# Three written-out engine orders replaced by others in a one-core attention kernel

## The chip, the cores and the metric

The kernel runs on one core of one Trainium2 chip. The metric is the device time of one execution in microseconds (us). Three timed runs of the kernel before gave 189.55, 189.56 and 189.82 us, with a median of 189.56 us.

## The reference

Cosine attention over 8 batches and 12 heads, 512 positions, head dimension 64, all in float32 in HBM:

```
Q_norm = Q / (norm(Q) + 1e-10);  K_norm = K / (norm(K) + 1e-10)
scores = Q_norm @ K_norm.T / tau            # tau = 0.1
weights = softmax(scores)                   # over the keys
out = weights @ V
```

## The kernel before

**Tiles.** Two neighbouring heads of one batch make a *pair*; there are 48 pairs, numbered 0 to 47. Each pair has four *chunks* of 128 keys, numbered 0 to 3. I write (42,2) for chunk 2 of pair 42. Each pair goes through these operations; the name in capitals is the key that the code gives it, and the line is where its instruction is issued.

- LD and LV (L311, L314): loads of Q, K and V, issued by SyncE.
- SQ (L337): GpSimd squares Q and K of a pair, one instruction of 128x1024.
- SSQ (L354) and RED (L361, L365): the sums of squares. For most pairs K's are first folded by eight matmuls with the identity (SSQ, written beside the outputs in one of the two `ops` banks of PSUM) and then reduced by a short VectorE instruction (L361). Q's are reduced by a long VectorE instruction alone (L365).
- NEW (L389 to L403): eight or nine small VectorE instructions that make 1/norm by Newton steps for a whole group of pairs at once. From pair 20 on a group has four pairs; group 18 is pairs 44 to 47. NEW18.7 is step 7 of group 18.
- SCL (L420): Q and K times 1/norm, to bf16. Q's (SCL s.0) on VectorE, K's (SCL s.1) mostly on GpSimd.
- TR (L426): four TensorE transposes each for Q (TR s.0) and K (TR s.1) into the one PSUM tile `tps`. EVA (L434): VectorE copies the tile to SBUF as `qt`. The next pair's TR can only start when EVA has emptied the tile.
- SCO (L508): two matmuls of 64x512 give the scores of one chunk for both heads, into one of two halves of `scps`. The halves alternate, so the scores of a chunk wait for the exponential of the chunk two before.
- EXP (L531): ScalarE's exponential of one chunk, 128x1024, from `scps` to `et`. For the last chunk of pair 47 there are three pieces (L522).
- VC (L536): GpSimd converts V to bf16 in `vb`, with a column of ones beside it.
- PV (L548; L576 for pair 47): the outputs. PV s.h.i is the group of four matmuls that sums head h and query tile i over the four chunks. It needs all four exponentials of its pair, VC, and an emptied `ops` bank.
- RCP and NRM (L559, L561): VectorE divides by the sums of weights and empties the bank. ST (L565): the store, issued by SyncE.

Two chunks, (37,3) and (45,3), get their exponential from a polynomial and not from ScalarE (function `poly`). Their scores (SCX, L468) go to `tps`; X (L473, L475) runs on VectorE; four steps Y s.0 to Y s.3 (L479, L480) on GpSimd; the last two, Y s.4 (L486) and Y s.5 (L480), on VectorE. Both of these last two read two tiles in SBUF.

**Order of the work.** Nothing in the program decides at run time. `P.add` collects 1831 operations in a list, and `ORDER` gives for each engine a string of indices into that list. `schedule` (L33) turns the strings into queues, and `run` (L43) writes each queue with a semaphore wait ahead of every operation whose inputs come from another engine. Each engine is strictly in order: an operation that waits holds up all behind it on its engine. How far operations may run ahead is set by the rings of buffers (L622): 15 pairs of Q, K and `vb`, 10 of V, 6 of squares, 4 of `qn`, `qt` and `et`, 8 of outputs.

A *slot* in what follows is TensorE's stretch between two neighbouring SCO in its queue; slot (42,2) is the one that ends with SCO of (42,2). The other TensorE work, PV, TR and SSQ, stands in slots.

Of the kernel before, what the change touches and what calls it, by code (L numbers as in the profile page):

```python
# [639 lines left out]
def slack(s, most):  # L640
# [14 lines left out]
    ),  # L655
    "pool": (
# [7 lines left out]
    ),  # L664
    "dve": (
# [24 lines left out]
    ),  # L690
# [33 lines left out]
    ),  # L724
    "act": (
# [44 lines left out]
```

## Time and profile before

| | |
|---|---|
| median of 3 runs | 189.56 us |
| the profiled execution's own time | 189.84 us |
| its span | 187.9 us |
| granted TensorE clock | 1.00 |
| ScalarE, TensorE, VectorE, GpSimd busy | 180.8, 173.7, 172.3, 166.8 us |
| HBM traffic | 50.3 MB, 268 GB/s over the span |

The page of the profile gives busy time by engine, the chain of work that ended last and the costliest groups. The timeline view lists single instructions or runs of equal ones as start, length, engine, line, operation, tiles and count; a bracket at the end tells idle time of the engine just before the row and who ended it. The records of one engine overlap: an instruction of ScalarE or VectorE is shown as started while the one before it still drains. So what an instruction occupies is read from start to start or from end to end, not from its length.

### The profile page before, as it was taken

The numbers are of one execution on the slowest core, as the hardware profiler recorded it, in microseconds if no ns is written. First come the engines' busy times: TensorE is split into PE (matmuls) and PEld (weight loads), VectorE is DVE, ScalarE is ACT, GpSimd is POOL, SyncE is SP. The second block draws the span as 40 slices with busy tenths as digits, with TensorE's granted clock in tenths as the row PEclk, the third lists the DMA queues.
The fourth block names the chain that finished last, engine by engine and source line by source line (L and its number), as shares of the span: only waits on it lengthen the run. The fifth ranks groups of instructions, "written<-read, shape, count | busy, mean of one in ns | idle before, by whom it ended". The sixth has DMA issues, their size and how long they took to land.

```text
span 187.9 us, 6635 instructions
## 1 busy us (share of the span) xinstructions
PE 173.7 (92%) x2694; PEld 108.7 (58%) x2694; DVE 172.3 (92%) x546; ACT 180.8 (96%) x212; POOL 166.8 (89%) x152
## 2 busy tenths in 40 slices
PE   6999999999998999999999999899999989999983
PEld 2655666566665666666666556556645446655552
DVE  2789999999999999999999999999999999988864
ACT  4799999999999999999999999999999999999992
POOL 4797999999999999999999999999999999696600
PEclk9999999999999999999999999999999999999999
DMA  4999999899999988999999999976996551312215
GB/s 148 356 350 349 348 354 331 233 328 370 379 385 375 326 243 264 333 304 297 361 379 381 380 380 301 306 244 198 302 336 194 173 167 59 112 59 76 95 59 169
DMA packets 52446, 50.76 MB, mean 270 GB/s; under 512 B 3136, under 2 KB 52416, under 8 KB 52416
## 3 DMA queue, kind: packets, MB, share of 16 engines
q1 hardware_dynamic: 51984, 50.02, 81.1%
q8 instruction: 21, 0.34, 0.8%
q10 hardware_dynamic: 432, 0.33, 0.5%
q14 instruction: 9, 0.07, 0.1%
HBM read 37.75 MB, written 12.58 MB: 268 GB/s over the span
## 4 chain that ended last, share of the span: by engine, by line
ACT 92%; PE 4%; DMA 1%; DVE 1%; issue 1%; POOL 0%
ACT et L531 90%; DMA qk<-in_Q_dram 1%; PE ops L548 1%; PE scps L508 1%; DVE xs L245 0%; PE ops L576 0%; ACT ys L379 0%; DVE ob L589 0%; PE scps L268 0%; POOL qn L258 0%; ACT nps L382 0%; PE tps L268 0%; ACT sq L239 0%; ACT et L522 0%; PE scps L194 0%
## 5 line engine op out<-in xcount | busy, mean ns | idle before, releaser
L531 ACT ACTIVATE et<-scps 128x1024 bf16<-128x1024 f32 (+1 forms) x191 | 174.3, 1151 | 0.5 <-PE scps L508 0.5
L337 POOL TENSOR_TENSOR sq<-qk 128x1024 bf16<-128x1024 f32 x44 | 82.7, 1893 | 1.4 <-DMA qk<-in_K_dram 1.2
L508 PE MATMUL scps<-qt 64*128 64x512 bf16 x380 | 75.2, 386 | 7.8 <-ACT et L531 4.4
L548 PE MATMUL ops<-vb,et 128*128 128x65 bf16 x1504 | 71.6, 194 | 1.1 <-DVE qn L420 0.5
L548 PEld LDWEIGHTS ops<-vb,et 128*128 128x128 bf16 x1504 | 55.1, 98 | 27.1 <-issue 17.4
L420 POOL TENSOR_TENSOR qn<-qk,rk 128x512 bf16<-128x512 f32 x36 | 37.2, 1042 | 2.8 <-DVE rk L394 2.5
L561 DVE TENSOR_TENSOR ob<-ops,rd 128x256 f32<-128x256 f32 x94 | 38.9, 417 | 0.4
L420 DVE TENSOR_TENSOR qn<-qk,nps 128x512 bf16<-128x512 f32 x58 | 38.5, 677 | 0.4 <-ACT nps L382 0.4
L434 DVE COPY qt<-tps 128x1024 bf16<-128x1024 bf16 x47 | 32.3, 687 | 2.6 <-PE tps L426 2.1
L426 PE MATMUL tps<-ident,qn 128*128 128x128 bf16 x376 | 33.9, 221 | 0.1
L508 PEld LDWEIGHTS scps<-qt 64*128 64x128 bf16 x380 | 18.9, 92 | 26.0 <-ACT et L531 11.8
L365 DVE TENSOR_REDUCE nps<-sq 128x8 f32<-128x512 bf16 x48 | 32.3, 683 | 0.0
L536 POOL TENSOR_SCALAR vb<-vf 128x512 bf16<-128x512 f32 x48 | 30.8, 655 | 0.2
L426 PEld LDWEIGHTS tps<-ident,qn 128*128 128x128 bf16 x376 | 21.4, 98 | 12.9 <-issue 6.6
L559 DVE RECIPROCAL rd<-ops 128x4 f32<-128x4 f32 x94 | 16.2, 176 | 3.3 <-PE ops L548 2.3
L354 PE MATMUL ops<-sq,ident 128*128 128x64 bf16 x368 | 18.5, 194 | 0.0
L354 PEld LDWEIGHTS ops<-sq,ident 128*128 128x128 bf16 x368 | 13.9, 98 | 4.1 <-issue 2.7
L361 DVE TENSOR_REDUCE nps<-ops 128x8 f32<-128x64 f32 x40 | 8.5, 213 | 0.6 <-PE ops L354 0.5
L389 DVE TENSOR_TENSOR nps<-nps,ys 128x32 f32<-128x32 f32 (+1 forms) x30 | 6.3, 209 | 0.1
L390 DVE SCALAR_TENSOR_TENSOR nps<-nps,ys 128x32 f32<-128x32 f32 (+1 forms) x30 | 6.2, 208 | 0.1
L480 POOL TENSOR_TENSOR xz<-xz 128x1024 f32<-128x1024 f32 x2 | 3.8, 1892 | 1.5 <-DVE xz L475 1.5
L191 PE MATMUL ops<-warm_in,ident 128*128 128x512 bf16 x8 | 3.6, 628 | 1.4 <-POOL ident L181 1.4
(61 smaller groups left out, 65.0 us busy)
## 6 DMA issues: line engine op xcount, KB each, us to landing
vf<-in_V_dram SPq DMA_DIRECT2D x48, 256.0 KB, 5.8
qk<-in_Q_dram SPq DMA_DIRECT2D x47, 256.0 KB, 5.0
qk<-in_K_dram SPq DMA_DIRECT2D x47, 256.0 KB, 5.7
out_dram<-ob SPq DMA_DIRECT2D x47, 256.0 KB, 3.9
qk<-in_Q_dram SPq DMA_DIRECT2D x2, 128.0 KB, 2.7
qk<-in_K_dram ACTq DMA_DIRECT2D x2, 128.0 KB, 2.9
out_dram<-ob SPq DMA_DIRECT2D x1, 128.0 KB, 1.7
out_dram<-ob ACTq DMA_DIRECT2D x1, 64.0 KB, 1.6
```

Source lines behind the costliest of these rows:

```text
L337: lambda e: e.tensor_tensor(out=sqf, in0=data, in1=data, op=ALU.mult))
L354: last = e.matmul(out=o_ps[bank][:, 320:384], lhsT=ident[:, :], rhs=sq[iqs][:, 8 * w : 8 * w + 8, 8 * k : 8 * k + 8], start=(k == 0), stop ...
L365: lambda e, w=w, dst=dst: e.tensor_reduce(out=dst, in_=sq[iqs][:, 8 * w : 8 * w + 8, :], axis=AX.X, op=ALU.add))
L420: lambda e, w=w, r=r: e.tensor_tensor(out=qn[iqn][:, w].rearrange("p t h d -> p h t d"), in0=qk[iq][:, w].rearrange("p h (t d) -> p h t d" ...
L426: last = e.transpose(t_ps[:, w, t, :], qn[iqn][:, w, t].rearrange("p h d -> p (h d)"), ident[:, :])
L434: lambda e: e.tensor_copy(out=qt[iqt][:, :, :, :].rearrange("p w t x -> p (w t x)"), in_=t_ps[:, :, :, :].rearrange("p w t x -> p (w t x)")))
L508: last = e.matmul(out=sc_ps[:, 2 * b + h, :], lhsT=qt[iqt][64 * h : 64 * h + 64, 1, c, :], rhs=qt[iqt][64 * h : 64 * h + 64, 0, :, :], sta ...
L531: lambda e, c=c, b=b, hs=hs: e.activation(out=et[iet][:, c, hs[0] : hs[-1] + 1, :], in_=sc_ps[:, 2 * b + hs[0] : 2 * b + hs[-1] + 1, :], f ...
L536: lambda e: e.tensor_scalar(out=vb[:, iq, :, :, 0:DIM].rearrange("p c h d -> p h c d"), in0=vf[iv][:, :, :].rearrange("p h (c d) -> p h c ...
L548: last = e.matmul(out=o_ps[h][:, 65 * t : 65 * t + 65], lhsT=et[iet][:, c, h, 128 * t : 128 * t + 128], rhs=vb[:, iq, c, h, :], start=(c = ...
L559: lambda e, h=h, grid=grid: e.reciprocal(out=rd[io][:, h, :], in_=grid[:, :, DIM]))
L561: lambda e, h=h, grid=grid: e.tensor_tensor(out=ob[io][:, h], in0=grid[:, :, 0:DIM], in1=rd[io][:, h, :].unsqueeze(2).to_broadcast([128, N ...
```

## The change

Three of the five strings in `ORDER` are replaced: those of GpSimd, VectorE and TensorE. SyncE's and ScalarE's strings, the operations themselves, their needs and all buffers stay as they are, and each new string has the same indices as the old one, in another order. In the queues the first difference is at SQ 21 on GpSimd, at NRM 12.0 on VectorE and at TR 15.0 on TensorE, some 58 to 62 us into the span; 79 of 148 places differ on GpSimd, 252 of 546 on VectorE and 419 of 735 on TensorE.

The change describes itself as orders of pairs 16 and later searched anew, with later scores and the lock of GpSimd and VectorE in the sum (that is, in the search's own cost), and with each query tile's values over all chunks in a row.

The diff, cut to parts that the prediction speaks of. GpSimd, around the polynomial of pair 37 (1436 to 1439 are Y37.0 to Y37.3; 1442, 1509, 1552 and 1476 are VC of pairs 37, 39, 40 and 38; 1684 is SCL 44.1):

```diff
-        "1176 1310 1459 1569 1210 1343 1603 1253 1526 1287 1386 1321 1397 1354 1421 1637 1670 1465 1712 1436 1437 "
-        "1438 1439 1476 1442 1509 1575 1552 1791 1586 1757 1609 1642 1740 1620 1684 1719 1653 1763 1774 1809 1695 "
-        "1796 1734 1735 1736 1737 "
+        "1493 1176 1242 1343 1310 1459 1569 1603 1397 1442 1526 1287 1386 1421 1637 1509 1321 1354 1465 1670 1712 "
+        "1436 1437 1438 1439 1552 1476 1575 1791 1609 1740 1757 1774 1642 1809 1695 1620 1586 1684 1719 1763 1796 "
+        "1653 1734 1735 1736 1737 "
```

TensorE, lines with pairs 40 to 42 (1612 is SCO (42,0), 1614 SCO (42,1), 1616 SCO (42,2); 1685 and 1683 are TR 44.1 and TR 44.0; 1553 to 1561 are PV of pair 40):

```diff
-        "1516 1517 1518 1519 1584 1641 1553 1643 1554 1612 1559 1560 1614 1555 1561 1562 1685 1683 1616 1556 1618 "
+        "1516 1517 1518 1519 1553 1584 1643 1641 1612 1554 1555 1559 1560 1561 1614 1685 1683 1616 1556 1562 1618 "
```

In the same way, slot by slot, with the operations named:

| slot | before | after |
|---|---|---|
| (26,1) | TR27.0, PV25.0.0, PV25.0.1 | PV24.1.2, PV24.1.3, TR27.0 |
| (28,2) | PV27.0.0 to 27.0.3, SSQ34.1 | PV27.1.0, PV27.0.0 |
| (30,1) | PV29.0.0, PV29.1.0 | TR31.1 |
| (40,2) | PV38.0.0 to 38.0.3, SSQ45.1 | PV38.0.0 to 38.0.3, SSQ45.1, PV38.1.0 |
| (40,3) | TR41.1, PV38.1.0 | nothing |
| (41,0) | five PV | six PV |
| (41,1) | PV39.0.3, PV38.1.3, SSQ46.1, TR42.1 | PV39.0.3, SSQ46.1 |
| (42,0) | TR43.0, PV40.0.0, TR43.1, PV40.0.1 | TR43.1, TR43.0 |
| (42,2) | PV40.0.2, PV40.1.2, PV40.1.3, TR44.1, TR44.0 | TR44.1, TR44.0 |
| (47,0) to (47,3) | 1, 5, 4 and 7 PV | 5, 4, 2 and 5 PV |

TR39.0 stands in slot (37,2) before and in (38,2) after, TR39.1 in (38,0) and in (38,1).

VectorE, around the polynomial of pair 37: before, EVA39, NEW17.7, SCL40.0, NEW17.8, RCP36.1, Y37.4, NRM36.1, RCP36.0, Y37.5; after, NEW17.7, NEW17.6, RED45.0, SCL40.0, EVA39, RCP36.1, Y37.4, NRM36.1, NEW17.8, Y37.5, RCP36.0. Further on, RCP38.1 moves ahead of RED46.1 (before, it stood behind it, inside the steps of NEW18), and EVA47 moves from ahead of Y45.4 to behind NRM44.0.

86 rows, old and new, of the table ORDER are left out of this document.

## The prediction, on record before the result

> **What bounds the kernel now.** I read the page first: busy shares, then the chain that ended last.
>
> ```profile
> span 187.9 us, 6635 instructions
> PE 173.7 (92%) x2694; PEld 108.7 (58%) x2694; DVE 172.3 (92%) x546; ACT 180.8 (96%) x212; POOL 166.8 (89%) x152
> ACT 92%; PE 4%; DMA 1%; DVE 1%; issue 1%; POOL 0%
> ACT et L531 90%; DMA qk<-in_Q_dram 1%; PE ops L548 1%; PE scps L508 1%; DVE xs L245 0%; PE ops L576 0%; ACT ys L379 0%; DVE ob L589 0%; PE scps L268 0%; POOL qn L258 0%; ACT nps L382 0%; PE tps L268 0%; ACT sq L239 0%; ACT et L522 0%; PE scps L194 0%
> ```
>
> ScalarE's exponentials are 90% of the chain, and no string of ScalarE changes. So the change can only remove time in which ScalarE waits for scores, and the end. How much is that? ScalarE's records overlap, so idle time doesn't show it; I take ends of EXP from the timeline and count them by the view of line L531.
>
> ```profile
> 53.37 1.26 ACT L531 ACTIVATE et<-scps 128x1024 bf16<-128x1024 f32 x1
> 82.70 1.26 ACT L531 ACTIVATE et<-scps 128x1024 bf16<-128x1024 f32 x1
> L531 ACT ACTIVATE et<-scps x33: 1245/1260/1281, 53.4 to 82.7; 128x1024 bf16<-128x1024 f32 x33
> 182.18 1.13 ACT L531 ACTIVATE et<-scps 128x1024 bf16<-128x1024 f32 x1
> L531 ACT ACTIVATE et<-scps x109: 1017/1122/1331, 82.7 to 182.2; 128x1024 bf16<-128x1024 f32 x109
> ```
>
> In the early stretch 33 EXP take 32 steps from end 54.63 to end 83.96: 29.33/32 = 0.9166 us each. I take this for ScalarE's own pace. The next 108 steps, to (47,2), end at 183.31. They take 99.35 us, where the pace gives 98.99. **Late scores cost 0.36 us in the whole changed stretch**, and that is all there is to win before the last chunk.
>
> **The change part by part.** *What makes scores late.* TensorE and ScalarE around (42,2), where before has its longest slot, and a slot with an SSQ for its price:
>
> ```profile
> 163.17 0.39 PE L508 MATMUL scps<-qt 64*128 64x512 bf16 x2
> 163.49 0.54 PE L548 MATMUL ops<-vb,et 128*128 128x65 bf16 x12
> 163.87 0.64 PE L426 MATMUL tps<-ident,qn 128*128 128x128 bf16 x8
> 164.44 0.39 PE L508 MATMUL scps<-qt 64*128 64x512 bf16 x2
> 163.84 1.02 ACT L531 ACTIVATE et<-scps 128x1024 bf16<-128x1024 f32 x1
> 164.87 1.02 ACT L531 ACTIVATE et<-scps 128x1024 bf16<-128x1024 f32 x1
> 92.72 0.39 PE L354 MATMUL ops<-sq,ident 128*128 128x64 bf16 x8
> 92.95 0.29 PE L548 MATMUL ops<-vb,et 128*128 128x65 bf16 x4
> ```
>
> From start to start, an SCO occupies 0.32, three PV 0.38 (0.125 each), and two TR 0.57 up to the next SCO. An SSQ takes 0.23. I split the 0.57 into 0.235 per TR and 0.10 of drain ahead of an SCO. So a slot takes 0.42 plus its other work, and at ScalarE's pace that leaves 0.50 for the work. More than that is carried over as lag. Here 0.375 + 0.47 = 0.845, on a lag from the slots before.
>
> How much lag is allowed? EXP (42,1) ends at 164.86 and EXP (42,2) at 165.89, 1.03 later: 0.11 late. This SCO started 1.45 before its EXP ended, so in time means at most 2 x 0.917 - 1.45 = 0.38 after the end of the EXP two before. That EXP ended at 164.86 - 0.917 = 163.94; SCO came 0.49 after: 0.49 - 0.38 gives the same 0.11.
>
> There is a second kind:
>
> ```profile
> 103.95 1.09 ACT L531 ACTIVATE et<-scps 128x1024 bf16<-128x1024 f32 x1
> 105.10 0.42 PE L548 MATMUL ops<-vb,et 128*128 128x65 bf16 x8 [0.20 <-DVE ys L394]
> 105.45 0.39 PE L508 MATMUL scps<-qt 64*128 64x512 bf16 x2
> ```
>
> In slot (26,1) two PV of pair 25 stand ahead of SCO. The profile puts the idle 0.20 down to VectorE, but the PV starts 0.06 after 105.04, when EXP (25,3) ends, which it needs. SCO then comes 0.41 after that end, 0.03 late. Slot (30,1) is built alike: 0.03 again. The remaining 0.36 - 0.11 - 0.06 = 0.19 I put to the other slots with 0.70 or more of work on a lag, (28,2), (41,1) and (42,0).
>
> *After.* Slots (26,1) and (30,1) hold no PV of the pair just exponentiated. With the prices above I carried the lag through every slot of the new TensorE order, from a smallest lag of 0.06. It passes 0.38 once: (40,2) has five PV and an SSQ, 0.06 + 0.86 - 0.50 = 0.42, late by 0.04. Slot (41,0) has six PV behind an empty slot: 0.31. All others stay below 0.33. **First term, if TensorE waits for nobody: -0.36 + 0.04 = -0.32.**
>
> *The end.*
>
> ```profile
> 181.26 1.13 ACT L531 ACTIVATE et<-scps 128x1024 bf16<-128x1024 f32 x1
> 182.06 1.02 PE L548 MATMUL ops<-vb,et 128*128 128x65 bf16 x28
> 183.02 0.39 PE L508 MATMUL scps<-qt 64*128 64x512 bf16 x2
> 183.45 1.15 ACT L522 ACTIVATE et<-scps 128x256 bf16<-128x256 f32 x3
> ```
>
> The last SCO stands behind seven PV and starts 0.63 after EXP (47,1) ends (182.39). The pieces start 0.14 after EXP (47,2) ends (183.31). After, the last four slots hold 5, 4, 2 and 5 PV: lags 0.19, 0.19, 0.06, 0.19, so the pieces wait for nothing. The gain is at least the idle 0.14. At most it is 0.14 plus the 0.21 by which a back-to-back EXP starts before its predecessor ends (1.13 - 0.917). **Second term: -0.25, the middle of 0.14 and 0.35.** The last PV, RCP, NRM and the store hang on these pieces and move with them; their operations and ScalarE's order of the pieces stay.
>
> *What is late next.* TR44 now opens slot (42,2) and no longer stands behind three PV. It needs SCL 44.1, and that needs NEW18.7:
>
> ```profile
> 159.59 0.23 DVE L361 TENSOR_REDUCE nps<-ops 128x8 f32<-128x64 f32 x1 [0.18 <-PE ops L354]
> 160.00 0.17 DVE L559 RECIPROCAL rd<-ops 128x4 f32<-128x4 f32 x1
> 160.12 0.23 DVE L389 TENSOR_TENSOR nps<-nps,ys 128x64 f32<-128x64 f32 x1
> 162.51 0.18 DVE L394 SCALAR_TENSOR_TENSOR rk<-nps,ys 128x32 f32<-128x32 f32 x1
> 162.77 1.04 POOL L420 TENSOR_TENSOR qn<-qk,rk 128x512 bf16<-128x512 f32 x1 [1.75 <-DVE rk L394]
> ```
>
> The row at 159.59 is RED46.1, 160.00 is RCP38.1, 162.51 is NEW18.7 and 162.77 SCL 44.1. GpSimd sat idle 1.75 us for NEW18.7, so four more VC ahead of SCL 44.1 (VC47, 44, 42, 41) fill idle time. SCL 44.1 ends at 163.81, and TR44.1 starts at 163.87 as shown above. If NEW18.7 comes no earlier, the SCO of (42,2) stays at 164.44. ScalarE would be ahead by then by 0.36 - 0.11 - 0.04 = 0.21, so its limit is 163.94 - 0.21 + 0.38 = 164.11: late by 0.33, and the first term is gone. If NEW18.7 comes 0.33 earlier, nothing is lost. RCP38.1 has left the steps of NEW18, which saves 0.12. Another 0.18 was RED46.1's wait for its SSQ, which now stands one PV further forward. But that counts only if VectorE itself is on time, and I doubt it:
>
> ```profile
> 133.21 1.79 POOL L536 TENSOR_SCALAR vb<-vf 128x512 bf16<-128x512 f32 x3
> 147.64 1.04 POOL L479 TENSOR_SCALAR xw<-xw 128x1024 f32<-128x1024 f32 x1
> 148.76 3.19 POOL L536 TENSOR_SCALAR vb<-vf 128x512 bf16<-128x512 f32 x3
> 149.15 1.30 DVE L486 SCALAR_TENSOR_TENSOR et<-xz,xw 128x1024 bf16<-128x1024 f32 x1
> 70.00:90.00 20.00, 19.44 (x319) 12.43 (x316) 19.50 (x64) 20.00 (x23) 19.91 (x19) 1.00 0.95 301
> 130.00:150.00 20.00, 18.44 (x277) 11.02 (x273) 19.92 (x61) 20.00 (x23) 19.66 (x17) 1.00 0.79 251
> 150.00:165.00 15.00, 14.06 (x229) 8.96 (x226) 14.39 (x43) 14.99 (x18) 13.25 (x14) 1.00 0.33 106
> 147.37 0.39 PE L508 MATMUL scps<-qt 64*128 64x512 bf16 x2
> 147.68 0.69 DVE L434 COPY qt<-tps 128x1024 bf16<-128x1024 bf16 x1
> 148.37 0.69 DVE L420 TENSOR_TENSOR qn<-qk,nps 128x512 bf16<-128x512 f32 x1
> ```
>
> (The two rows with ranges are from the view of stages: the third busy time is VectorE, the fifth GpSimd.) VC37 and VC39 move ahead of Y37.0. GpSimd has no idle time to speak of there, so Y37.3 moves by two VC, 2 x 0.60 = 1.2, from 147.64 to 148.84, and ends at 149.88. VectorE reaches Y37.4 at 149.15 now; it would wait 0.73. Queued behind it are Y37.5, NRM36.0, EVA40 and all else of VectorE; PV37 waits for Y37.5. EVA39 (147.68 now) also waits: TR39.0 stands one slot past the SCO after the one at 147.37, so it starts at about 147.37 - 0.11 + 0.92 + 0.32 = 148.5, and EVA39 some 0.4 later. SCL40.0 (148.37) and NEW17.7 move ahead of it, 0.7 together, so its place in the queue comes at 147.68 + 0.7, and about 0.5 is waited there. That lies inside the 0.73. VectorE is 19.92 of 20.00 busy up to 150, so none of it is hidden; from 150 to 165 it has 15.00 - 14.39 = 0.61 of idle time to catch up in. That leaves it about 0.1 late, with RED46.1's 0.18 used up. I take NEW18.7 as 0.10 earlier, near the 0.12 of the one row that is certain to go: SCO (42,2) at 164.34, late by 0.23. **Third term: +0.23, between 0 and 0.33, or more if VectorE falls further behind.**
>
> *The lock.* Three VC that meet Y37.4 and Y37.5 take 3.19, three without company 1.79: 1.4 us of GpSimd. Y37.4 and Y37.5 stay where they are, so VC40 and VC38 pay it in place of VC37 and VC39; I count nothing, and SCL 44.1's idle 1.75 covers it. The Trainium skill, page "SBUF — State Buffer", section "Who interferes with whom", says that a VectorE instruction with two SBUF inputs and a GpSimd one that reads SBUF exclude each other, and that the one issued first keeps the ports. The trace agrees for VectorE first. By that rule VC40, which can start when Y37.3 ends, could also be first; see the rivals.
>
> *Nothing else.* Other pairs' VC, SQ and SCL change places by up to some microseconds within rings of 6 to 15; SyncE's string is the same and its loads run many pairs ahead. I cost them at nothing. If that cover fails, one stall of an EXP costs what the late slots above cost, 0.03 to 0.11.
>
> **Sum.** -0.32 - 0.25 + 0.23 = -0.34 against the profiled execution's own 189.84 (span 187.9): 189.50. The median of the runs, 189.56, lies 0.28 below that execution; on its scale 189.2.
>
> **The rivals.** A difference of 0.2%, 0.38 us, is about what a measurement can tell from none: bounds 189.18 and 189.94.
>
> - *A, the forecast*, 189.2: 0.42. It straddles the bound, since the third term may be 0.1 less.
> - *B, no wait at TR44*, because VectorE gains more before pair 37 than I see: -0.57, 189.0. For it: VectorE's 0.5 us of idle between 70 and 90 may shrink. Against: 19.92 of 20 from 130 on. 0.24.
> - *C, the wait takes the place of the late scores*: NEW18.7 as now or a little later; only the end is won, and part of that goes: 189.45. 0.13.
> - *D, the lock falls to GpSimd*: VC40 first, Y37.4 later by one VC, 0.60, and all of it handed on to TR44: -0.34 + 0.60 = +0.26, 189.8. Against: VectorE's wait ends at once with Y37.3, while in the rows GpSimd's next instruction starts 0.08 after Y37.3 ends (148.68 to 148.76). 0.07.
> - *E, slower: VectorE becomes the bound.* Place: Y37.4 to NEW18.7. If the 0.73 is not caught up at all, NEW18.7 comes about 0.75 later than now and TR44 holds SCO (42,2) by that much more: third term 0.33 + 0.75 = 1.08 against gains of 0.57, +0.5, 190.05. It decides from NEW18.7 0.24 later than now (162.75 in place of 162.51) on, and over 0.2% slower from 0.62 later. 0.14.
>
> That the orders don't run as written can't be: queues are in order.
>
> **Chances.** Faster: B 0.24 and half of A, 0.45. Within: half of A, C and D, 0.41. Slower: E, 0.14. The range takes in B to D, 188.9 to 189.8.
>
> **What would show it.** EXP of (26,1) and (30,1) one pace apart; slots (28,2), (41,1), (42,0) without delay; the last SCO less than 0.38 after EXP (47,1) ends, and no idle time ahead of the three pieces; VectorE idle before Y37.4 by 0.5 to 0.8; TR44.1 waiting for GpSimd. I'm wrong if VectorE has large waits before pair 37, if TR44 finds SCL 44.1 done, or if a slot of 0.5 or less is late.

## The result, and the profile after

The change took 189.37 us in the median of 22 runs (188.66 to 189.90), the kernel before 189.71 us in 22 runs on the same chip (189.25 to 190.68). The ratio over paired rounds is **0.9973, with a 95% interval from 0.9961 to 0.9985**: 0.51 us faster, between 0.28 and 0.74. (The two medians stand 0.34 apart, inside that interval.)

The page of the changed kernel, the same four lines as before (its profiled execution took 189.78 us of its own, at a granted clock of 0.995):

```profile
span 187.8 us, 6632 instructions
PE 173.9 (93%) x2694; PEld 108.4 (58%) x2694; DVE 173.0 (92%) x546; ACT 180.4 (96%) x212; POOL 166.7 (89%) x152
ACT 93%; DMA 3%; SPq 1%; issue 1%; PE 1%; DVE 1%
ACT et L531 92%; DMA qk<-in_Q_dram 3%; PE ops L576 1%; SPq L311 0%; SPq L308 0%; DVE ob L589 0%; ACT sq L329 0%; ACT ys L379 0%; ACT nps L382 0%; DVE rd L587 0%; PE tps L576 0%
```

The chain is still ScalarE's exponentials. The line `PE scps L508 1%` of before is gone from it: no exponential on the chain waits for its scores long enough to be listed. The load of Q has 3% where it had 1%, and this comes from the first microseconds, which the change doesn't touch; the last section comes back to it. The span fell by only 0.1, because this execution began slower. So I compare *steps* again: ends of EXP in the timeline of ScalarE, and their count in the view of line L531.

```profile
83.06 1.20 ACT L531 ACTIVATE et<-scps 128x1024 bf16<-128x1024 f32 x1
182.31 1.11 ACT L531 ACTIVATE et<-scps 128x1024 bf16<-128x1024 f32 x1
L531 ACT ACTIVATE et<-scps x109: 1018/1197/1302, 83.1 to 182.3; 128x1024 bf16<-128x1024 f32 x109
```

From the end of EXP (20,0), 84.26, to that of (47,2), 183.42, the 108 steps take 99.16, and at the pace of 0.9166 they would take 98.99. **Late scores cost 0.17 us now, where they cost 0.36.** The changed stretch starts 0.30 later than in before's profile (84.26 against 83.96); times of after are meant less 0.30 wherever I say "on before's clock".

The end, ScalarE's last instructions and then TensorE's:

```profile
181.39 2.03 ACT L531 ACTIVATE et<-scps 128x1024 bf16<-128x1024 f32 x2
183.21 1.25 ACT L522 ACTIVATE et<-scps 128x256 bf16<-128x256 f32 x3
```

```profile
181.97 0.78 PE L548 MATMUL ops<-vb,et 128*128 128x65 bf16 x20
182.68 0.39 PE L508 MATMUL scps<-qt 64*128 64x512 bf16 x2
```

The last SCO stands behind five PV, not seven. The first piece starts at 183.21, 0.21 ahead of the end of EXP (47,2) at 183.42; before, it started 0.14 behind that end. From the end of EXP (47,2) to the end of the span it takes 187.80 - 183.42 = 4.38 us now, and 187.94 - 183.31 = 4.63 before: 0.25 less.

The middle, where TR44 opens slot (42,2): TensorE, then GpSimd, then VectorE.

```profile
163.44 0.39 PE L508 MATMUL scps<-qt 64*128 64x512 bf16 x2
163.98 0.62 PE L426 MATMUL tps<-ident,qn 128*128 128x128 bf16 x8 [0.15 <-POOL qn L420]
164.53 0.39 PE L508 MATMUL scps<-qt 64*128 64x512 bf16 x2
```

```profile
162.88 4.04 POOL L420 TENSOR_TENSOR qn<-qk,rk 128x512 bf16<-128x512 f32 x4 [0.35 <-DVE rk L394]
```

```profile
159.69 0.23 DVE L361 TENSOR_REDUCE nps<-ops 128x8 f32<-128x64 f32 x1
159.83 0.17 DVE L559 RECIPROCAL rd<-ops 128x4 f32<-128x4 f32 x1
...
161.88 0.23 DVE L389 TENSOR_TENSOR nps<-nps,ys 128x64 f32<-128x64 f32 x1
...
162.35 0.22 DVE L390 SCALAR_TENSOR_TENSOR nps<-nps,ys 128x64 f32<-128x64 f32 x1
162.60 0.19 DVE L394 SCALAR_TENSOR_TENSOR rk<-nps,ys 128x32 f32<-128x32 f32 x1
```

The wait at TR44 is there: TensorE sits idle for SCL 44.1 (the first of the four at 162.88), and GpSimd for NEW18.7 (162.60), and that goes back to RED46.1 (159.69). But it is short.

This table has all profiles of this study. "Late" is the sum of what the ends of EXP from (13,0) to (47,2) lose to the pace, with the places where more than 0.015 is lost; "end" is the time from the end of EXP (47,2) to the end of the span; "ratio" is the timed one, with its interval.

| kernel | late | where | end | span | ratio |
|---|---|---|---|---|---|
| before | 0.36 | (26,1) 0.03, (28,2) 0.06, (30,1) 0.03, (41,1) 0.10, (42,0) 0.04, (42,2) 0.11 | 4.63 | 187.94 | |
| the change | 0.17 | (40,2) 0.08, (42,2) 0.07, (43,3) 0.02 | 4.38 | 187.80 | 0.9973 [0.9961, 0.9985] |
| e1_tail_alone | 0.37 | the six of before | 4.39 | 187.22 | 0.9989 [0.9974, 1.0003] |
| e2_middle_alone | 0.85 | (40,2) 0.13, (42,2) 0.14, (43,3) 0.02, (45,2) 0.55 | 4.64 | 188.11 | 1.0030 [1.0014, 1.0046] |
| e3_whole_again | 0.17 | (40,2) 0.08, (42,2) 0.07, (43,3) 0.02 | 4.40 | 187.09 | 0.9987 [0.9971, 1.0003] |
| e4_tensor_order_alone | about 20 | dozens of places | | 207.6 | 1.1032 [1.0979, 1.1084] |
| e5_scores_ahead | 0.30 | (28,2) 0.06, (41,1) 0.10, (42,0) 0.04, (42,2) 0.11 | 4.64 | 188.31 | 1.0004 [0.9990, 1.0019] |
| e6_middle_alone_mended | 0.17 | (40,2) 0.08, (42,2) 0.06, (43,3) 0.02 | 4.64 | 187.51 | 0.9988 [0.9974, 1.0001] |
| e7_gpsimd_first | 2.78 | (39,2) 1.26, (39,3) 0.82, (40,2) 0.32, five others | 4.39 | 190.09 | 1.0083 [1.0052, 1.0114] |
| e8_norm_steps_sooner | 0.30 | (40,2) 0.08, (42,2) 0.13, (43,1) 0.03, (43,3) 0.05 | 4.39 | 187.27 | 0.9982 [0.9969, 0.9994] |
| e9_ssq46_sooner | 0.15 | (42,2) 0.13, (43,3) 0.02 | 4.38 | 187.08 | 0.9981 [0.9963, 0.9999] |
| e10_tr39_sooner | 0.14 | (42,2) 0.12, (43,3) 0.02 | 4.38 | 190.29 | 0.9981 [0.9964, 0.9997] |

In the profiled execution of e10_tr39_sooner the granted clock was 0.69 from 10 to 20 us and some 3 us were lost there, so only what lies behind EXP (13,0) is used of it.

So by steps the change is worth -0.19 in the middle and -0.25 at the end, **-0.44 us**.

### The profile page after: what moved, and what is told of

It reads as the page before. It is cut to its first block, busy times and chain, and to the rows that moved or that the text cites. A ratio compares the mean times of both kernels' runs of the same rounds, so it can differ in the third digit from the quotient of the medians.

```text
span 187.8 us, 6632 instructions
## 1 busy us (share of the span) xinstructions
PE 173.9 (93%) x2694; PEld 108.4 (58%) x2694; DVE 173.0 (92%) x546; ACT 180.4 (96%) x212; POOL 166.7 (89%) x152
## 4 chain that ended last, share of the span: by engine, by line
ACT 93%; DMA 3%; SPq 1%; issue 1%; PE 1%; DVE 1%
ACT et L531 92%; DMA qk<-in_Q_dram 3%; PE ops L576 1%; SPq L311 0%; SPq L308 0%; DVE ob L589 0%; ACT sq L329 0%; ACT ys L379 0%; ACT nps L382 0%; DVE rd L587 0%; PE tps L576 0%
## 5 line engine op out<-in xcount | busy, mean ns | idle before, releaser
L531 ACT ACTIVATE et<-scps 128x1024 bf16<-128x1024 f32 (+1 forms) x191 | 174.1, 1170 | 0.0
L508 PE MATMUL scps<-qt 64*128 64x512 bf16 x380 | 75.2, 386 | 7.3 <-ACT et L531 3.5
L548 PE MATMUL ops<-vb,et 128*128 128x65 bf16 x1504 | 73.4, 194 | 0.1
L548 PEld LDWEIGHTS ops<-vb,et 128*128 128x128 bf16 x1504 | 55.7, 98 | 28.7 <-issue 21.1
L508 PEld LDWEIGHTS scps<-qt 64*128 64x128 bf16 x380 | 18.8, 92 | 24.9 <-ACT et L531 11.7
L536 POOL TENSOR_SCALAR vb<-vf 128x512 bf16<-128x512 f32 x48 | 30.3, 646 | 0.2
L331 POOL TENSOR_TENSOR sq<-qk 128x512 bf16<-128x512 f32 (+1 forms) x4 | 3.7, 932 | 2.0 <-DMA qk<-in_K_dram 2.0
```

What stands on the lines that cost most here:

```text
L508: last = e.matmul(out=sc_ps[:, 2 * b + h, :], lhsT=qt[iqt][64 * h : 64 * h + 64, 1, c, :], rhs=qt[iqt][64 * h : 64 * h + 64, 0, :, :], sta ...
L531: lambda e, c=c, b=b, hs=hs: e.activation(out=et[iet][:, c, hs[0] : hs[-1] + 1, :], in_=sc_ps[:, 2 * b + hs[0] : 2 * b + hs[-1] + 1, :], f ...
L536: lambda e: e.tensor_scalar(out=vb[:, iq, :, :, 0:DIM].rearrange("p c h d -> p h c d"), in0=vf[iv][:, :, :].rearrange("p h (c d) -> p h c ...
L548: last = e.matmul(out=o_ps[h][:, 65 * t : 65 * t + 65], lhsT=et[iet][:, c, h, 128 * t : 128 * t + 128], rhs=vb[:, iq, c, h, :], start=(c = ...
```

## The experiments

The theory: end and middle are two separate gains; the middle's is what the slots of TensorE save, less the wait at TR44, which hangs on NEW18.7 and, further back, on Y37.4. One rival is that the whole gain is the end, the wait at TR44 having taken the place of the late scores. Another is about Y37.4: it may be late because of the lock with GpSimd, or only because VectorE has more work ahead of it.

The diffs give a queue's order in names of operations in place of indices. `before[:677]` is the first 677 places of before's queue. Times of experiments that are set beside the change's are shifted to before's clock by the end of EXP (20,0), and are then called "aligned".

### The end alone

TensorE's queue from place 678 on and VectorE's from place 526 on as in the change; the rest, with all of GpSimd, as before.

```diff
 TensorE
-before[:677] + before[677:]
+before[:677] + after[677:]
 VectorE
-before[:525] + before[525:]
+before[:525] + after[525:]
```

> Before's orders up to the scores of (44,3) on TensorE and up to NRM 43.0 on VectorE, the new orders from there; GpSimd as before (its two orders end alike). Theory (the gain is two separate things, late scores in the middle and the last four slots): the late scores stay near 0.36 us from EXP (13,0) to EXP (47,2), the stretch from the end of EXP (47,2) to the end of the span shrinks from 4.63 to about 4.38 us, and the time falls by 0.25 us, 0.13%. Rival (the end is only faster because VectorE and GpSimd have run ahead in the middle): the end gains less than 0.1 us, or EVA47, which now stands behind Y45.5, holds up the scores of (47,0) and late scores grow by 0.1 or more.

The end of ScalarE in this kernel:

```profile
181.72 1.11 ACT L531 ACTIVATE et<-scps 128x1024 bf16<-128x1024 f32 x1
182.62 1.25 ACT L522 ACTIVATE et<-scps 128x256 bf16<-128x256 f32 x3
```

The pieces start 0.21 ahead of the end of EXP (47,2) (182.83), as in the change; the end takes 4.39, and the late scores are before's, 0.37. So the end gives 0.24 by itself and nothing of the middle. The timed ratio, -0.11% with an interval that touches 1, agrees with -0.13% but wouldn't tell it.

### The middle alone, first cut

```diff
 TensorE
-before[:677] + before[677:]
+after[:677] + before[677:]
 VectorE
-before[:525] + before[525:]
+after[:525] + before[525:]
 GpSimd
-before
+after
```

> The reverse: the new orders up to those same places, before's end. Theory: late scores fall from 0.36 to about 0.17 us, the end stays at 4.63 us, the time falls by 0.19 us, 0.10%; with e1_tail_alone this adds up to the whole change. Rival (all of the gain is the end): late scores as before and no difference. Rival (the middle gains more than the late scores tell, for the timed runs gave 0.51 us in all): 0.3 us or more.

It was slower, 1.0030, and neither theory had that. TensorE ahead of the place that the table shows:

```profile
175.13 0.54 PE L548 MATMUL ops<-vb,et 128*128 128x65 bf16 x12 [0.80 <-DVE ob L561]
```

The cut itself made this. At the seam, VectorE's order has EVA46 ahead of NRM 43.1, and before's TensorE order wants the bank of NRM 43.1 for its PV ahead of TR 46.0, for which EVA46 waits: 0.80 of idle TensorE and 0.55 of late scores at (45,2). It says nothing on the change. One thing in it is of use: a load reached SQ29 0.21 later in this execution, GpSimd ran 0.20 later from there on, and Y37.4 ended 0.19 later. (40,2) then lost 0.13 in place of 0.08, and (42,2) 0.14 in place of 0.07. So what happens at Y37.4 does reach both places.

### The middle alone, mended

The same with one exchange at the seam:

```diff
 VectorE
-EVA 46, NRM 43.1, RCP 43.0
+NRM 43.1, EVA 46, RCP 43.0
```

> As e2_middle_alone, with NRM43.1 ahead of EVA46 in VectorE's string, as before has it. There EVA46 waited for TR46.0, which before's TensorE order issues late, and held up NRM43.1, PV44.1.0 and so the scores of (45,2) by 0.55 us. Theory: that one goes; late scores of 0.17 us, or up to 0.28 where GpSimd has lost 0.2 us to a late load; the end stays at 4.63 us; time 0.1 to 0.2 us below before. Rival (the middle of the new orders gains nothing): late scores of 0.36 us or more.

Late 0.17, at the change's three places, and before's end:

```profile
180.83 2.05 ACT L531 ACTIVATE et<-scps 128x1024 bf16<-128x1024 f32 x2
183.02 0.38 ACT L522 ACTIVATE et<-scps 128x256 bf16<-128x256 f32 x1
```

EXP (47,2) ends at 182.88 and the first piece starts 0.14 behind it, as before. The middle alone gives -0.19, the end alone -0.24, and the sum, -0.43, is the change's -0.44 to within 0.01. (The timed ratios alone can't tell these parts from each other or from the whole; the steps of the profiles do.) That the whole gain is the end is out: it would leave the late scores at 0.36.

### The whole change again

The change's three orders, unaltered.

> The whole change once more. Late scores 0.17 us, with the two large ones again at (40,2), 0.08, and (42,2), 0.07 us; the end 4.38 us; the time 0.25 to 0.75 us below before. If the late scores are an accident of one execution, they come out at other places or by 0.1 us or more different in sum.

The late scores came out at the same three places, each within 0.002 us of the first profile, with a sum of 0.174 against 0.173. The span, though, was 187.09 against 187.80. So the steps repeat to a few ns, and spans don't.

### TensorE's order alone

```diff
 TensorE
-before
+after
```

> Only TensorE's string is new; VectorE's and GpSimd's are before's. Theory (TensorE's slots decide, but TensorE's new places need VectorE's and GpSimd's new ones): TensorE waits at transposes and emptied banks, late scores of 0.5 to 3 us, slower than before by up to 1.5%. Rival (the gain is TensorE's order alone, and the other two strings are idle decoration): late scores 0.2 us or less and the same time as the whole change.

It lost 10.3%, some 20 us: far more than expected. Two rows of its waits (columns: total, times, longest):

```profile
ACT et L531 <- PE scps L508: 16.3, 21, 2.7
...
PE ops L548 <- DVE ob L561: 11.7, 15, 1.6
```

PV in the new order want banks that VectorE, in the old order, empties later, and its NRM and RCP stand behind operations that want TensorE. The three strings are one order: TensorE's, taken whole, can't be kept by itself.

### Scores ahead of the PV of the pair just done

Before, with only two moves: the SCO of (26,1) and of (30,1) go ahead of the PV that wait for the EXP that ended last.

```diff
 TensorE
-TR 27.0, PV 25.0.0, PV 25.0.1, SCO 26.1, PV 25.0.2
+TR 27.0, SCO 26.1, PV 25.0.0, PV 25.0.1, PV 25.0.2
...
-SCO 30.0, PV 29.0.0, PV 29.1.0, SCO 30.1, PV 29.0.1
+SCO 30.0, SCO 30.1, PV 29.0.0, PV 29.1.0, PV 29.0.1
```

> Before with two operations moved in TensorE's string: SCO (26,1) ahead of PV25.0.0 and SCO (30,1) ahead of PV29.0.0. Theory (those PV wait for the exponential that SCO waits for too, and hold SCO up): both late scores of 0.03 us vanish, late scores fall from 0.36 to 0.30 us, nothing else moves; in time 0.06 us, less than the timed runs can tell. Rival (what the profile names, VectorE ended TensorE's idle time): both stay.

Both places are gone from the list, the four others stand as they were, and the sum fell from 0.36 to 0.30. So the second kind of late scores is what the prediction said, 0.03 each. The timed ratio, 1.0004 [0.9990, 1.0019], can't see 0.06 us.

### GpSimd given a long instruction after the polynomial's fourth step

The change, with SQ47 (1.89 us) in place of VC40 behind Y37.3, so that a longer instruction meets Y37.4.

```diff
 GpSimd
-Y 37.3, VC 40, VC 38, SCL 41.1, SQ 47.0, SCL 42.1
+Y 37.3, SQ 47.0, VC 40, VC 38, SCL 41.1, SCL 42.1
```

> The whole change with one move on GpSimd: SQ47 (1.85 us long) stands ahead of VC40, VC38 and SCL41.1, right behind Y37.3. It starts 0.3 us before VectorE comes to Y37.4, as VC40 does in the change. Lock theory (an instruction of GpSimd that has started keeps VectorE's two-input instruction out for its whole length): Y37.4 ends about 1.06 us after SQ47 ends, as it ended 1.06 after VC40 in both profiles at hand; that is some 1.25 us later than in the change; PV37 waits for Y37.5, and scores of (39,2) are late by 0.7 to 1.1 us. Rival (Y37.4 was only long because it runs beside GpSimd, or VectorE takes the ports when it comes): Y37.4 takes 1.2 to 1.4 us, late scores stay within 0.1 us of 0.17, and SQ47 is the long one.

GpSimd, VectorE and TensorE there:

```profile
150.00 2.93 POOL L337 TENSOR_TENSOR sq<-qk 128x1024 bf16<-128x1024 f32 x1
```

```profile
149.98 1.20 DVE L486 SCALAR_TENSOR_TENSOR et<-xz,xw 128x1024 bf16<-128x1024 f32 x1
...
151.53 1.95 DVE L480 TENSOR_TENSOR et<-et,xp 128x1024 bf16<-128x1024 bf16 x1
```

```profile
153.54 0.93 PE L548 MATMUL ops<-vb,et 128*128 128x65 bf16 x16 [1.03 <-DVE et L480]
```

The loss is larger than expected (late 2.78 in all, 1.26 of it at (39,2), where I had 0.7 to 1.1; ratio 1.0083), and it was made at another instruction than I thought. Y37.4 started at 149.98, 0.02 ahead of SQ47, and took a clean 1.20. SQ47 was held: 2.93 in place of 1.89. So Y37.4 did not meet a running SQ47; the next one did. Y37.5 was issued at 151.53 into the running SQ47 and took 1.95, where it takes 0.68 in the change; it ended 0.55 after SQ47 did (153.48 against 152.93). PV of pair 37 waited 1.03 for it, and the scores of (39,2) came 1.26 late. That is against the rival, by which VectorE takes the ports when it comes. So the lock works in both directions, and which side pays was decided here by 0.02 us.

Not all of this is the moved instruction's. Late scores of 0.29 in all, at (28,1), (33,1), (34,0) and (34,2), come ahead of it. Two squares on GpSimd waited for loads of K in this execution, one of them 0.17 us and the other as shown:

```profile
102.05 1.89 POOL L337 TENSOR_TENSOR sq<-qk 128x1024 bf16<-128x1024 f32 x1 [0.41 <-DMA qk<-in_K_dram]
```

Aligned, Y37.3 ended 0.67 later than in the change and Y37.4 started 0.30 later. That is why SQ47 came just behind Y37.4 and not 0.3 ahead of it.

### NEW18.7 sooner by a filler taken away

The change, with NRM 39.1 moved from inside the steps of NEW18 to behind them.

```diff
 VectorE
-NEW 18.4, NRM 39.1, NEW 18.5, NEW 18.7, NEW 18.6, EVA 43
+NEW 18.4, NEW 18.5, NEW 18.7, NEW 18.6, NRM 39.1, EVA 43
```

> The whole change with NRM39.1 (0.33 us of VectorE) moved from between steps 4 and 5 of NEW18 to behind step 6. Theory (the scores of (42,2) hang on NEW18.7, SCL44.1 and TR44.1): NEW18.7 comes 0.2 us sooner, SCL44.1 and TR44.1 as well, the late 0.066 us at (42,2) goes, (40,2) keeps its 0.08; late scores of 0.11 us in all. Rival (TensorE's queue alone makes (42,2) late): NEW18.7 sooner, (42,2) unchanged.

NEW18.7 came 0.21 sooner, as expected, and yet (42,2) got worse, 0.13 in place of 0.07. VectorE, then TensorE:

```profile
161.20 0.23 DVE L389 TENSOR_TENSOR nps<-nps,ys 128x64 f32<-128x64 f32 x1
161.46 0.23 DVE L390 SCALAR_TENSOR_TENSOR nps<-nps,ys 128x64 f32<-128x64 f32 x1
...
161.94 0.41 DVE L561 TENSOR_TENSOR ob<-ops,rd 128x256 f32<-128x256 f32 x1
162.27 0.68 DVE L434 COPY qt<-tps 128x1024 bf16<-128x1024 bf16 x1
162.87 0.67 DVE L420 TENSOR_TENSOR qn<-qk,nps 128x512 bf16<-128x512 f32 x1
```

```profile
163.21 0.79 PE L426 MATMUL tps<-ident,qn 128*128 128x128 bf16 x8
```

From NEW18.4 (161.20) to NEW18.5 (161.46) it now takes 0.26; in the change, with NRM 39.1 between, 162.35 - 161.88 = 0.47. So taking the NRM out saves 0.21 there. Behind the steps it takes 0.33 (161.94 to 162.27). Everything after it comes 0.12 later, and one of these is SCL 44.0 (162.87, ends 163.54), which TR 44.0 needs. The two TR take 0.79 here and 0.62 in the change: TR 44.1 starts sooner, TR 44.0 has to wait within. Two dependent steps leave a gap in which a short instruction is partly free; the filler was where it cost least.

### SSQ46.1 and the scores of (40,2) sooner

The change, with PV 38.1.0 out of slot (40,2) and SSQ46.1 first in its slot.

```diff
 TensorE
-SSQ 45.1, PV 38.1.0, SCO 40.2, SCO 40.3, PV 38.1.1, PV 39.0.0, PV 39.0.1, PV 38.1.2, PV 39.0.2, PV 38.1.3, SCO 41.0, PV 39.0.3, SSQ 46.1
+SSQ 45.1, SCO 40.2, PV 38.1.0, PV 38.1.1, PV 38.1.2, SCO 40.3, PV 39.0.0, PV 39.0.1, PV 39.0.2, PV 38.1.3, PV 39.0.3, SCO 41.0, SSQ 46.1
```

> The whole change with TensorE's slots (40,2) to (41,1) filled otherwise: PV38.1.0, 38.1.1 and 38.1.2 in the empty slot (40,3), PV39.0.3 at the end of (41,0), so that SSQ46.1 opens (41,1). Slot prices: (40,2) 0.73 of work, its late 0.08 us goes. Theory (TR44 at (42,2) is a wall that VectorE's NEW18 steps set, and what is won ahead of it is given back there): SSQ46.1 comes 0.12 us sooner, but VectorE reaches RED46.1 only 0.04 sooner, so NEW18.7 comes 0.04 sooner and (42,2) is late by about 0.11 in place of 0.066; late scores 0.13 to 0.15 us in all. Rival (the two late scores are independent): 0.09 us. Time 0.03 to 0.08 us below the change, less than the timed runs can tell.

(40,2) is gone, and (42,2) grew from 0.07 to 0.13; the sum is 0.15. TensorE at TR44:

```profile
163.26 0.62 PE L426 MATMUL tps<-ident,qn 128*128 128x128 bf16 x8 [0.15 <-POOL qn L420]
```

TR44.1 starts, aligned, at 163.66, where it starts at 163.68 in the change. SSQ46.1 ended 0.09 sooner, and RED46.1 came 0.01 sooner (159.39): VectorE, busy with what stands ahead, can't take it earlier. What ScalarE wins at (40,2) it gives back at a place that comes when NEW18.7 lets it.

### TR39.0 sooner

The same, and TR 39.0 one slot earlier, so that EVA39 and with it Y37.4 come sooner on VectorE.

```diff
 TensorE
-TR 39.1, PV 36.1.0, PV 36.1.1, SCO 38.1, TR 39.0, PV 36.1.2
+TR 39.1, TR 39.0, PV 36.1.0, SCO 38.1, PV 36.1.1, PV 36.1.2
```

> e9_ssq46_sooner with TR39.0 one slot sooner, (38,1), so that EVA39 doesn't wait. Lock theory: VectorE reaches Y37.4 0.1 us sooner, but VC40 has begun on GpSimd 0.2 us before, so Y37.4 still ends 1.06 us after VC40 ends, nothing behind it moves, and late scores are those of e9_ssq46_sooner within 0.02 us. Rival (EVA39's wait is what makes VectorE late, as the prediction's third term had it): all of VectorE behind Y37.4 is 0.1 us sooner, NEW18.7 too, and (42,2) is late by 0.1 us less.

VectorE and GpSimd at Y37.4:

```profile
152.42 1.51 DVE L486 SCALAR_TENSOR_TENSOR et<-xz,xw 128x1024 bf16<-128x1024 f32 x1
```

```profile
152.24 0.63 POOL L536 TENSOR_SCALAR vb<-vf 128x512 bf16<-128x512 f32 x1
```

Aligned, Y37.4 starts at 149.60, 0.11 sooner than in the change, and ends at 151.11, no sooner. It ends 1.06 after VC40 (153.93 against 152.87). So VectorE's queue is not what holds it; the lock is. Late: 0.14. This kernel and the one above are at most 0.03 us better than the change by steps, and their ratios, 0.9981 both, can't be told from the change's 0.9973 or from 0.9987 of its repetition.

## Why the prediction came out right, point by point

It gave -0.34 us; the steps of the profile give -0.44, and the timed runs -0.51 (0.28 to 0.74). What separates -0.44 from -0.51 is smaller than the interval.

**The bound and the pace** held: 0.9166 us an EXP from (13,0) to (20,0) in all profiles but that of e4_tensor_order_alone, which already waits there, and all that was won is late scores and the end.

**First term, -0.36 + 0.04.** All six late places of before are gone, as the prices by slot said. (40,2) was the one new place that they gave, 0.04, and it cost 0.08. The other 0.04 was brought along from two slots before. An EXP and, behind it, the scores that wait for it:

```profile
153.58 1.26 ACT L531 ACTIVATE et<-scps 128x1024 bf16<-128x1024 f32 x1
154.98 0.39 PE L508 MATMUL scps<-qt 64*128 64x512 bf16 x2
```

SCO (40,0) started 0.14 after EXP (39,2) ended (154.84), where the walk had its smallest lag of 0.06; so SCO (40,1) had a lag of 0.10, and (40,2) one of 0.46. SCO (40,0) waits for an EVA and for an EXP, with no TensorE operation ahead of it that has already waited for that EVA. From pair 20 on the change has eleven such SCO and before nine, and none started sooner than 0.144 after its EXP; among the others the least is 0.054. The walk had one smallest lag for all. Y37.4 has no part in this: SCO (39,2), behind the first PV of pair 37, started 0.057 after its EXP. It reached (40,2) in the first cut of the middle, where that lag was 0.23.

**Second term, -0.25**: 4.63 became 4.38, and e1_tail_alone has 4.39 with nothing else changed. The estimate was the middle of 0.14 and 0.35, and 0.14 + 0.21 is indeed the shift of the pieces' start against the end of EXP (47,2). The end moved by less than that, by 0.25, because the three pieces take 1.25 from first start to last end where they took 1.15, and end 1.04 after EXP (47,2) (184.46) where they ended 1.29 after it (184.60). The bounds were worked out; that their middle was hit is luck, for nothing in the working favoured it.

**Third term, +0.23: this step was mis-sized.** It measured 0.07 at (42,2), and 0.02 at (43,3) that I hadn't foreseen. SCO (42,2) came at 164.23 on before's clock and not at 164.34, and ScalarE was 0.04 less far ahead, which takes 0.23 down to 0.08. The chain was right: TR44.1 waits for SCL 44.1, that for NEW18.7. What failed is "I take NEW18.7 as 0.10 earlier, near the 0.12 of the one row that is certain to go". On before's clock NEW18.7 came at 162.30, 0.21 earlier (162.51), and not by that row. From RED46.1 to NEW18.7 it takes 162.60 - 159.69 = 2.91, and before 162.51 - 159.59 = 2.92: RCP38.1 left and another RCP stands there (159.83). All of the gain is RED46.1 itself, 159.39 on before's clock against 159.59. That is its wait for SSQ46.1, the 0.18 that I had struck out since VectorE would be late by then. The row at 159.69 shows no wait any more. VectorE came there just when the SSQ was done, and e9_ssq46_sooner shows that it could not have come earlier: not late, and not early either.

Why wasn't it late? GpSimd of the changed kernel around the polynomial, and VectorE at Y37.4:

```profile
143.45 1.89 POOL L480 TENSOR_TENSOR xz<-xz 128x1024 f32<-128x1024 f32 x1
...
148.54 1.04 POOL L479 TENSOR_SCALAR xw<-xw 128x1024 f32<-128x1024 f32 x1
149.66 0.62 POOL L536 TENSOR_SCALAR vb<-vf 128x512 bf16<-128x512 f32 x1
```

```profile
148.02 0.68 DVE L365 TENSOR_REDUCE nps<-sq 128x8 f32<-128x512 bf16 x1
148.61 0.68 DVE L420 TENSOR_TENSOR qn<-qk,nps 128x512 bf16<-128x512 f32 x1
149.31 0.69 DVE L434 COPY qt<-tps 128x1024 bf16<-128x1024 bf16 x1
149.92 0.17 DVE L559 RECIPROCAL rd<-ops 128x4 f32<-128x4 f32 x1
150.01 1.34 DVE L486 SCALAR_TENSOR_TENSOR et<-xz,xw 128x1024 bf16<-128x1024 f32 x1
...
151.71 0.68 DVE L480 TENSOR_TENSOR et<-et,xp 128x1024 bf16<-128x1024 bf16 x1
```

The step before it, "Y37.3 moves by two VC, 2 x 0.60 = 1.2", was too large: 148.54 - 0.30 - 147.64 = 0.60. I moved the two VC and left what stood further ahead as it was. Before, GpSimd had idle time there:

```profile
92.60 1.04 POOL L420 TENSOR_TENSOR qn<-qk,rk 128x512 bf16<-128x512 f32 x1 [0.46 <-DVE rk L394]
```

Before has 0.67 of idle time on GpSimd from its first changed operation to Y37.0, this 0.46 and two short waits. After, it has one wait, 0.23. That accounts for 0.44 of the 0.60 by which Y37.3 came sooner than I thought; the rest I haven't traced. On VectorE the work that moved ahead of Y37.4 (RED45.0, 0.6 from start to start) fills the time: the rows follow each other without a gap, but for 0.1 ahead of EVA39, and Y37.3 (ends 149.58) has been done for 0.43 when Y37.4 starts. **VectorE does not wait for Y37.3 at all**, where the prediction had 0.73. Rival B's reason, that VectorE gains more than I saw, was right in part; its price of no wait at TR44 was not.

**The lock**, counted as nothing, is rival D's mechanism, and it happened; but it had happened before the change too. VC40 started at 149.66, 0.35 ahead of Y37.4, and Y37.4 took 1.34. Its clean length is 1.20 (in e7_gpsimd_first, and Y45.4 of before, which has no GpSimd beside it), so the lock cost 0.14, not the 0.60 that D had for a whole VC, because most of VC40 was over. In before, VC38 stands behind Y37.3:

```profile
148.76 0.62 POOL L536 TENSOR_SCALAR vb<-vf 128x512 bf16<-128x512 f32 x1
```

It is the first of the three VC that the prediction shows as one row of 3.19. It began 0.39 ahead of Y37.4 (149.15), which took 1.30: the lock cost 0.10 there. So "the trace agrees for VectorE first" holds for the VC behind it alone, and the change added 0.04, near the nothing that was counted. In the seven profiles in which VC40 is first, Y37.4 ends 1.06 after VC40 ends, whether it starts at 149.60 or 149.71, and in before, e1_tail_alone and e5_scores_ahead it ends 1.06 after VC38 does. The reason given against D, that VectorE would follow Y37.3 at once, fell with the wait. The Trainium skill, page "SBUF — State Buffer", section "Who interferes with whom", has it that the one issued first keeps the ports. The traces agree in both directions, though not to the whole length: VC40 first, 1.34 and 1.51 for Y37.4, which ends 1.06 after VC40 with 1.20 of its own; Y37.4 first, 2.93 for SQ47 in place of 1.89. Little of the 0.14 reached the sum, since NEW18.7 hangs on RED46.1, and that on TensorE's SSQ.

**Rivals C and E** are out: VectorE was ready for RED46.1 when its SSQ was, and the late scores were not replaced by the wait. **Nothing else** held but for the 0.02 at (43,3). That slot holds two PV and one of the two SCX of pair 45, less than 0.5 of work, so the sign "a slot of 0.5 or less is late" showed there. TensorE's SCX waited 0.27 for VectorE's X:

```profile
168.93 0.39 PE L468 MATMUL tps<-qt 64*128 64x512 bf16 x1 [0.27 <-DVE xz L475]
```

With the measured terms the sum is -0.36 + 0.08 - 0.25 + 0.09 = -0.44: two errors, of 0.04 and of 0.14, of opposite sign.

## What to carry to other kernels

When the bound engine's own order stays, count only its steps over its pace and the end, and walk the lag slot by slot; that gave the first term to within 0.04 us, and bounds that held for the second. When an operation moves on an engine that is nearly full, re-time the whole queue ahead of it, since waits further up vanish and pay for it; the one term that I took from local rows was wrong by 0.16 at its place. Look for what each gain runs into: the moves that helped (40,2) were given back at (42,2), because that place hangs on another chain.

## What the runs showed of the hardware that was not expected

**The first EXP, not the change, sets the spread of the spans.** The view of line L531 over the whole span, in e1_tail_alone and then in e5_scores_ahead, whose heads are identical:

```profile
L531 ACT ACTIVATE et<-scps x191: 579/1144/1337, 8.0 to 181.7; 128x1024 bf16<-128x1024 f32 x187, 128x512 bf16<-128x512 f32 x4
```

```profile
L531 ACT ACTIVATE et<-scps x191: 579/1157/1331, 8.9 to 182.5; 128x1024 bf16<-128x1024 f32 x187, 128x512 bf16<-128x512 f32 x4
```

The first EXP starts at 8.0 and at 8.9, and EXP (13,0) ends at 57.81 and at 58.71. ScalarE's wait ahead of its third square, in the change's timeline:

```profile
6.85 0.63 ACT L329 ACTIVATE sq<-qk 128x512 bf16<-128x512 f32 x1 [1.01 <-DMA qk<-in_Q_dram]
```

It waits 1.01 for a load of Q there, 0.97 in e5_scores_ahead, and 0.12 in e1_tail_alone. It is not always this load: in e7_gpsimd_first ScalarE doesn't wait there, but 0.67 and 0.91 at two other squares, and the first EXP starts at 8.51. A late start of up to 0.9 us stays in the span, and that is more than the change is worth, while late scores of the repeated change agree to 0.002 us. For a change behind the head, steps from a fixed EXP tell in one profile what spans of single executions can't.

**A two-input VectorE instruction that meets a GpSimd one is not simply delayed by its rest.** In ten profiles Y37.4 ended 1.06 after the VC that was first, though it takes 1.20 alone: about 0.14 of it passes while it is held.

**Scores that wait for two engines start later than scores that wait for one.** Behind the end of their EXP the least is 0.144 in the one case and 0.054 in the other, in before and in the change. Why, no run here shows.
